# Two transformer blocks on one core: gates and branch projections computed with the weights as the moving operand

## The chip, the cores and the metric

The kernel runs on one core of a Trainium2 chip. The metric is the device time of one execution in microseconds (us); the median of three runs is compared. Engines are called TensorE (PE, with its weight loads PEld), VectorE (DVE), ScalarE (ACT), GpSimd (POOL) and SyncE (SP).

## What the kernel must compute

The input is x of 256 rows (tokens) by 2048 columns. It passes two blocks. In each, x is normed and projected by one wide matrix into queries, keys, values and gate logits; several attentions each give a branch output o, which is projected back to 2048 columns; the branches are gated and summed, projected once more, normed and added to x. Then a feed-forward part follows. All data are float32. Cut to what matters here:

```python
# block 1: two branches, each of width 1024
gates = sigmoid(gate_logits + b_gate)                     # 256 x 4096
mixed = (g_sb * (o_sb @ w_o_sb) + g_mla * (o_mla @ w_o_mla)) @ w_out
h = h + rms_norm(mixed, norm_post_mix)
# block 2: three branches, each of width 512; gates 256 x 6144
bias = take(rel_bias_table, rel_bucket(q_pos - k_pos))    # one row of numbers per head, by distance
logits = q @ k.T * scale + bias                           # 20 heads, masked by distance
mix = ga * (ya @ w_oa) + gb * (yb @ w_ob) + gc * (yc @ w_oc)
x = x + rmsnorm(mix @ w_out, post_mix_g)
```

## The kernel before

Every weight matrix is streamed once from DRAM in pieces of [128 x 1024] float32 (512 KB), in the order of use, seven pieces ahead, by SyncE's queue (`load_piece`). Each piece is split three pieces ahead of its use into a rounded part `hi` (ScalarE, line 335) and a rest `lo` (VectorE, line 336), because TensorE multiplies a rounded float32 format; activations are split in the same way (`split_act`). A product is then hi x hi + lo x hi + hi x lo.

The work is a list of `Group`s, each a block of output columns. `run` takes them in order, piece by piece: it loads and splits ahead, multiplies, and after each piece steps the generators that evacuate earlier groups (`tail_step`) and the side generators that compute attention heads (`step`). All engines execute their instructions in the order in which this list writes them.

`multiply` has two forms. In kind "w" the weights are the stationary operand and the activations move: a piece holds 4 k-tiles of 256 output columns and gives 16 matmuls, in pairs of 512 moving columns (`hi` against both parts) and 256 (`lo` against the rounded part). The result lies in PSUM turned, with the output columns on the partitions. In kind "a" the activations stand and the weights move: a piece holds 2 k-tiles of 512 output columns and gives 12 matmuls of 512 columns; the result has the tokens on the partitions.

Before the change the gates and the branch projections are of kind "w". A gate group is evacuated by `gather` (per 256 columns two copies on ScalarE, line 851, and two additions on VectorE, line 852), scaled by the norm on GpSimd (line 860) and later turned into a sigmoid with its bias on ScalarE (`sigmoids`, line 1022). A branch group goes through `gather` too (tile `y`), is multiplied by its gate on GpSimd (line 1035) and added to the branch before it, on GpSimd as well (line 1039); the sum (tile `tr`) is then split for the output projection (`hh`, `hl`). A group of block 1's branches has four pieces, one of block 2's a single piece. PSUM holds four such result banks, two for a group, so that a group can begin when the one before the last is evacuated.

In block 2 the attention bias is one row of 384 numbers per head. `bias_rows` (run during the last down projection group of block 1) writes each row 128 times into DRAM, and `bias_tile` reads it with a row step of 383, so that each query gets its row shifted by one more place.

`renorm` adds a norm's result to x, transposes x and starts the next projection. While TensorE waits for the norm, `warm_forms` issues twelve matmuls on zeros, at the first of three norms with 128 columns, at the other two with 512 and 256 in turn.

Of the kernel before, what the change touches and what calls it, by code (L numbers as in the profile page):

```python
# [19 lines left out]
P = 128  # L20
# [24 lines left out]
G_BUFS = 63  # L45
# [47 lines left out]
def lay_out(x):  # L93
# [6 lines left out]
        + span(2048, 2) + span(0, 4, 256) + span(1024, 4, 256) + span(4416, 16, 256),  # L100
        moving=range(5),
# [5 lines left out]
    g.add("osb", x["w_o_sb"][0], span(0, 8, 256))  # L107
    g.add("omla", x["w_o_mla"][0], span(0, 8, 256))
# [11 lines left out]
        + span(2304, 4, 256) + span(3328, 1) + span(3840, 24, 256),  # L120
        moving=(4, 12),
    )
    g.add("oa", x["w_oa_2"][0], span(0, 8, 256))
    perm = [h for i in range(4) for h in (i, 4 + i)]
    ob = x["w_ob_2"][0].reshape(8, 64, D)[perm].reshape(512, D)
    g.add("ob", ob, span(0, 8, 256))
    g.add("oc", x["w_oc_2"][0], span(0, 8, 256))
# [11 lines left out]
    for name, v in [  # L139
        ("pre1", x["norm_pre_mix"][0]), ("qn", x["q_norm"][0]), ("kvn", x["kv_norm"][0]),  # L140
        ("ffn1", x["norm_pre_ffn"][0]), ("pre2", x["pre_mix_g_2"][0]), ("ffn2", x["pre_ffn_g_2"][0]),
        ("bg1", x["b_gate"][0]), ("bg2", x["b_gate_2"][0]), ("sub", x["diff_subln_g_2"][0]),
        ("cb", x["conv_b_2"][0]), ("cw0", x["conv_w_2"][0, 0]), ("cw1", x["conv_w_2"][0, 1]),
        ("cw2", x["conv_w_2"][0, 2]),
    ]:
        c = column(v)
        where[name] = n
        n += c.shape[1]
        cols.append(c)
    a["colv"] = np.ascontiguousarray(np.concatenate(cols, axis=1))  # L150
    a["rows"] = np.ascontiguousarray(
# [68 lines left out]
class Net:  # L220
    def __init__(self, ctx, tc, dram, sizes, colpos, out):
# [15 lines left out]
        self.norms = 0  # L237
# [186 lines left out]
class Blocks(Net):  # L424

    def setup(self):
# [26 lines left out]
        self.idle_r = self.const([P, 512], "idle_r", F32R)  # L453
        nc.vector.memset(self.idle_r.bitcast(F32), 0.0)
# [14 lines left out]

    def warm_forms(self, which):  # L470

        t = self.idle_r
        ps = self.aux("warm")
        two = lambda x: x.rearrange("p (r b) -> p b r", r=2)
        out = lambda x: x.rearrange("p (b r) -> p b r", r=2)
        plain = [t[:, 0:P], t[:, P : 2 * P]]
        turned = [t[:, a : a + 2 * P].rearrange("p (b r) -> p r b", r=2)[:, 0] for a in (0, P)]
        full, half, few = two(t), two(t)[:, 0:P], two(t)[:, 0:64]
        jobs = [
            [(plain[i % 2], few, P) for i in range(6)] + [(turned[i % 2], few, P) for i in range(6)],  # L480
            [(plain[i % 2], (full, half)[i % 2], (512, T)[i % 2]) for i in range(12)],
            [(turned[i % 2], (full, half)[i % 2], (512, T)[i % 2]) for i in range(12)],
        ][which]
        for i, (lhs, rhs, n) in enumerate(jobs):
            self.nc.tensor.matmul(out(ps[:, 0:n]), lhsT=lhs, rhs=rhs, start=i == 0, stop=i == 11, skip_group_check=True)
# [31 lines left out]
    def broadcast_r(self, diag, qscale):  # L517
# [59 lines left out]
    def renorm(self, first, gname, qscale, update=True, twin=None):  # L577
# [38 lines left out]
        def broadcast():  # L616
            diag = self.diagonal(self.rpre)
            yield
            self.broadcast_r(diag, qscale)
            self.r_ready = True  # L620
# [97 lines left out]
    def turn(self, e):  # L718
# [6 lines left out]
        nc.vector.tensor_copy(pt, ps[:, 0:384])  # L725
# [28 lines left out]
    def bias_tile(self, h):  # L754
        m = self.mpool.tile([P, T], F32, tag="m", name=self.name("m"))
        src = bass.AP(self.bias.tensor, self.bias.offset + h * P * 384 + 127, [[383, P], [1, T]])
        self.nc.gpsimd.dma_start(m, src)
        return m

    def diff_head(self, h):  # L760
# [20 lines left out]
        w = self.turn(es[0])  # L781
# [19 lines left out]
    def soft_pair(self, qs, ks, masks, vs, out, i, name, floors=None, sinks=None):  # L801
# [17 lines left out]
        for j in range(2):  # L819
            ws.append(self.turn(es[j]))  # L820
            yield
# [20 lines left out]
    def gather(self, ps, name, scale=None, n=2):  # L842
# [3 lines left out]
        for i in range(n):  # L846
# [15 lines left out]
    def gathered(self, ps, name, rb, n=2):  # L862

        o = self.gather(ps, name, n=n)
# [6 lines left out]
    def evac_cols(self, store, i, mult):  # L871

        def f(ps):
            if mult is None or isinstance(mult, float):
                o = self.gather(ps, "tr", mult)
            else:
                o = yield from self.gathered(ps, "tr", mult)
# [138 lines left out]
    def sigmoids(self, gates, bname, n):  # L1016

        for p in range(n):
            while ("pair", p) not in gates:
# [3 lines left out]
            if p % 2:  # L1023
                yield

    def branch_evac(self, b, j, nb, gates):
# [3 lines left out]
        def evac(ps):  # L1030
            p = 8 * b + j
            g = gates["pair", p]
            y = self.gather(ps, "y")
            yield
            nc.gpsimd.tensor_tensor(g, g, y, op=OP.mult)  # L1035
# [6 lines left out]
            yield  # L1042
            self.split_pair(g, self.mix, j)
# [53 lines left out]
    def mix_out(self, branches, gates, key_out, row):  # L1097
# [3 lines left out]
        for j in range(8):  # L1101
            for b, (key, o) in enumerate(branches):
                gs.append(Group(key, j, lambda k, o=o: o[k], self.branch_evac(b, j, len(branches), gates)))
# [4 lines left out]
    def block1(self):  # L1108
# [28 lines left out]
        gs[-1].after = lambda: self.add_side(heads + [self.sigmoids(gates, "bg1", 16)])  # L1137
        gs += [Group("in1", 13 + i, u, self.evac_cols(gates, i, self.rbc)) for i in range(16)]
# [7 lines left out]
    def bias_rows(self):  # L1146
# [13 lines left out]
        self.bias = self.tc.dram_tile([20, P, 384], F32, name="bias")  # L1160
        nc.gpsimd.dma_start(self.bias, mask[0:20, None, 0:384].to_broadcast([20, P, 384]))
# [33 lines left out]
    def block2(self):  # L1195
# [24 lines left out]
        def mobas():  # L1220
# [5 lines left out]
            self.add_side(gens + [self.sigmoids(gates, "bg2", 24)])  # L1226

        gs = [
            Group("in2", 0, u, self.evac_cols(dq, 0, self.rbq)),
            Group("in2", 1, u, self.evac_cols(dq, 1, self.rbq)),  # L1230
# [3 lines left out]
            Group("in2", 5, u, self.evac_cols(sq, 0, self.rbq)),  # L1234
            Group("in2", 6, u, self.evac_cols(sq, 1, self.rbq)),
            Group("in2", 7, u, self.evac_sw, after=windows),
            Group("in2", 8, u, self.evac_cols(bq, 0, self.rbq)),
            Group("in2", 9, u, self.evac_cols(bq, 1, self.rbq)),
# [4 lines left out]
        self.renorm(gs[0], "pre2", -0.125, twin=gs[1])  # L1243
        gs += [Group("in2", 13 + i, u, self.evac_cols(gates, i, self.rbc)) for i in range(24)]
# [34 lines left out]
```

## Time and profile before

| | before |
|---|---|
| median of three runs | 2639.85 us (2639.09 to 2640.11) |
| the profiled execution | 2639.83 us, its span 2638.1 us |
| TensorE busy | 2599.4 us, 99% of the span |
| VectorE busy | 1719.2 us, 65% |
| ScalarE busy | 1410.7 us, 53% |
| GpSimd busy | 499.0 us, 19% |
| DRAM read | 510.35 MB, 196 GB/s over the span |

The span is the time from the first to the last instruction; the rest of the execution's time lies around it. Records of matmuls overlap, since they are pipelined, so a busy TensorE is not one at its peak: the distance from one start to the next tells more than the length of a record.

### The profile page before, as it was taken

How to read it: one execution, taken by the hardware profiler on the slowest of the kernel's cores; microseconds unless marked ns; L12 is line 12 of the kernel's file. 1: busy time of each engine (PE TensorE's matmuls, PEld its weight loads, DVE VectorE, ACT ScalarE, POOL GpSimd, SP SyncE). 2: the span in 40 equal slices, each digit the busy share in tenths (PEclk: the TensorE clock that was granted, in tenths of full speed). 3: DMA queues.
4: the chain of work that ended last, by engine and by line, in shares of the span. 5: the costliest groups of instructions: out<-in, count | busy, mean ns of one | idle time of the engine just before them, and what ended most of it. 6: DMA issues, size and time to landing. Idle time of an engine off the chain costs nothing.

```text
span 2638.1 us, 38603 instructions
## 1 busy us (share of the span) xinstructions
PE 2599.4 (99%) x14802; PEld 2337.2 (89%) x14802; DVE 1719.2 (65%) x2187; ACT 1410.7 (53%) x2189; POOL 499.0 (19%) x371
## 2 busy tenths in 40 slices
PE   9999999999999999999999999998999999999997
PEld 7898899988999999888889889997889999998886
DVE  6656666856666666544467676568578788786454
ACT  5547465546555555444355456555466666665443
POOL 0010011401222222200021111129123222221000
PEclk9999999999999999999999999999999999999999
DMA  7665556675666666766755665665756666666664
GB/s 242 195 191 161 163 176 199 201 222 169 200 202 202 198 204 201 223 208 202 246 178 173 190 197 183 202 195 171 223 155 215 204 202 201 201 202 220 202 200 150
DMA packets 144777, 518.91 MB, mean 197 GB/s; under 512 B 16980, under 2 KB 17390, under 8 KB 144592
## 3 DMA queue, kind: packets, MB, share of 16 engines
q1 hardware_dynamic: 140544, 505.07, 61.8%
q0 software_dynamic: 3904, 11.37, 1.6%
q8 instruction: 115, 1.88, 0.3%
q14 instruction: 70, 0.57, 0.1%
q10 hardware_dynamic: 144, 0.01, 0.0%
HBM read 510.35 MB, written 6.03 MB: 196 GB/s over the span
## 4 chain that ended last, share of the span: by engine, by line
PE 89%; issue 4%; POOL 3%; DVE 2%; DMA 1%; ACT 1%; SPq 0%; DVEq 0%; ACTq 0%; POOLq 0%
PE mm L421 86%; POOL tr L1035 1%; POOL tr L1039 1%; DMA raw<-w_dn 1%; PE s L689 1%; DVE lo L336 1%; PE o L675 0%; PE tr L543 0%; PE pt L723 0%; DVE res L572 0%; ACT hi L335 0%; POOL res L575 0%; DMA raw<-w_in 0%; PE o L676 0%; ACT u L536 0%
## 5 line engine op out<-in xcount | busy, mean ns | idle before, releaser
L336 DVE TENSOR_TENSOR lo<-raw,hi 128x1024 fp32r<-128x1024 f32 (+1 forms) x957 | 1293.0, 1353 | 738.0 <-ACT hi L335 735.3
L421 PE MATMUL mm<-u,hi 128*128 128x512 f32 x4704 | 1554.6, 384 | 0.2
L335 ACT CAST hi<-raw 128x1024 fp32r<-128x1024 f32 (+1 forms) x957 | 998.6, 1047 | 763.8 <-PE mm L421 634.7
L421 PE MATMUL mm<-u,lo 128*128 128x256 f32 x4704 | 1283.0, 273 | 0.7 <-DVE lo L336 0.7
L421 PEld LDWEIGHTS mm<-u,hi 128*128 128x128 f32 x4704 | 889.8, 189 | 125.7 <-issue 1.0
L421 PEld LDWEIGHTS mm<-u,lo 128*128 128x128 f32 x4704 | 903.7, 192 | 1.4 <-DVE lo L336 1.3
L421 PE MATMUL mm<-hi,h 128*128 128x512 f32 x1408 | 419.8, 379 | 0.6 <-ACT hi L335 0.6
L421 PEld LDWEIGHTS mm<-hi,h 128*128 128x128 f32 x1408 | 266.1, 189 | 38.7 <-ACT hi L335 1.0
L421 PE MATMUL mm<-lo,h 128*128 128x512 f32 x704 | 267.3, 380 | 2.7 <-DVE lo L336 2.7
L851 ACT COPY low<-mm 128x256 f32<-128x256 f32 x382 | 132.2, 374 | 170.8 <-PE mm L421 169.6
L860 POOL TENSOR_TENSOR tr<-tr,rbc 128x512 f32<-128x512 f32 x48 | 63.4, 1320 | 541.8 <-DVE tr L852 541.8
L421 PEld LDWEIGHTS mm<-lo,h 128*128 128x128 f32 x704 | 133.0, 189 | 23.4 <-DVE lo L336 4.5
L421 PE MATMUL mm<-hi,u 128*128 128x512 f32 (+1 forms) x448 | 133.2, 374 | 1.4 <-ACT hi L335 1.4
L1082 POOL TENSOR_TENSOR cc<-cc 128x256 f32<-128x256 f32 x44 | 68.2, 1550 | 292.9 <-DVE cc L1075 262.6
L492 POOL TENSOR_TENSOR r<-st,mhalf 128x2 f32<-128x2 f32 x14 | 11.8, 849 | 576.5 <-DVE st L491 576.5
L860 POOL TENSOR_TENSOR gu<-gu,rbc 128x512 f32<-128x512 f32 x44 | 57.4, 1306 | 244.1 <-DVE gu L852 241.2
L421 PE MATMUL mm<-lo,hh 128*128 128x512 f32 x256 | 97.1, 379 | 0.0
L421 PE MATMUL mm<-hi,hh 128*128 128x512 f32 x256 | 97.0, 379 | 0.0
L421 PE MATMUL mm<-hi,hl 128*128 128x512 f32 x256 | 97.0, 379 | 0.0
L421 PEld LDWEIGHTS mm<-hi,u 128*128 128x128 f32 x448 | 83.8, 191 | 12.4 <-ACT hi L335 2.1
L421 PE MATMUL mm<-lo,u 128*128 128x512 f32 (+1 forms) x224 | 83.2, 371 | 1.1 <-DVE lo L336 1.1
L1075 DVE SCALAR_TENSOR_TENSOR cc<-cu,colv,cc 128x255 f32<-128x255 f32 (+1 forms) x176 | 81.2, 483 | 3.1
(224 smaller groups left out, 2010.4 us busy)
## 6 DMA issues: line engine op xcount, KB each, us to landing
raw<-w_in SPq DMA_DIRECT2D x284, 512.0 KB, 4.2
raw<-w_gu SPq DMA_DIRECT2D x176, 512.0 KB, 4.3
raw<-w_dn SPq DMA_DIRECT2D x176, 512.0 KB, 4.3
raw<-w_up SPq DMA_DIRECT2D x176, 512.0 KB, 4.2
raw<-w_out SPq DMA_DIRECT2D x64, 512.0 KB, 4.3
raw<-w_osb SPq DMA_DIRECT2D x16, 512.0 KB, 4.2
raw<-w_omla SPq DMA_DIRECT2D x16, 512.0 KB, 4.1
raw<-w_ukv SPq DMA_DIRECT2D x8, 512.0 KB, 4.3
```

The costliest lines, as they stand in the source:

```text
L335: self.nc.scalar.copy(hi[:, :n], raw[:, :n])
L336: self.nc.vector.tensor_tensor(lo[:, :n], raw[:, :n], hi[:, :n].bitcast(F32), op=OP.subtract)
L421: self.nc.tensor.matmul(out, lhsT=lhs, rhs=rhs, start=start, stop=stop, skip_group_check=True)
L492: self.nc.gpsimd.tensor_tensor(r, y, self.mhalf[:, 0:w], op=OP.pow)
L689: nc.tensor.matmul(s[:, c : c + w], lhsT=q[:, qs], rhs=k[:, 0:w], start=start and i == 0, stop=i == n - 1, skip_group_check=True,)
L851: nc.scalar.copy(lc, b)
L860: self.nc.gpsimd.tensor_tensor(o3, o3, rb[:, None, :].to_broadcast([P, n, T]), op=OP.mult)
L1035: nc.gpsimd.tensor_tensor(g, g, y, op=OP.mult)
L1039: nc.gpsimd.tensor_tensor(g, g, gates["pair", p - 8], op=OP.add)
L1075: nc.vector.scalar_tensor_tensor(cn[:, s:T], un[:, 0 : T - s], self.col(w, k), cn[:, s:T], op0=OP.mult, op1=OP.add)
L1082: nc.gpsimd.tensor_tensor(g, g, v, op=OP.mult)
```

## The change

Gates and branch projections become kind "a", with 512 columns to a group; their weights are laid out for that on the host. A gate group is evacuated by VectorE alone, which scales by the norm and adds the gate bias; the bias is loaded as a row broadcast to all partitions when the group starts, on GpSimd's queue. A branch group is evacuated by VectorE alone, which multiplies PSUM by the gate. The sum over branches stays on GpSimd. Since the sum now has tokens on the partitions, TensorE turns it by transposes for the output projection. The bias rows of block 2 are written once, and `bias_tile` reads them with a row step of 1; for that the queries of these heads are stored in reverse order, and the attention weights are put back in order when they are turned. `warm_forms` gives way to `warm(12)`, which has twelve bf16 matmuls of 512 columns. The pool of general tiles grows from 63 to 64.

```diff
-        + span(2048, 2) + span(0, 4, 256) + span(1024, 4, 256) + span(4416, 16, 256),
-        moving=range(5),
+        + span(2048, 2) + span(0, 4, 256) + span(1024, 4, 256) + span(4416, 8),
+        moving=(*range(5), *range(13, 21)),
...
-    g.add("osb", x["w_o_sb"][0], span(0, 8, 256))
+    g.add("osb", x["w_o_sb"][0], span(0, 4), moving=range(4))
...
-                self.warm_forms(self.norms)
-                self.norms += 1
+                self.warm(12)
...
-            nc.vector.tensor_scalar(self.rbq, ps[:, 0:T], qscale, None, op0=OP.mult)
+            form = lambda x: x.rearrange("p (t b) -> p t b", t=NT)
+            nc.vector.tensor_scalar(form(self.rbq)[:, :, ::step], form(ps[:, 0:T]), qscale, None, op0=OP.mult)
...
-        nc.vector.tensor_copy(pt, ps[:, 0:384])
+        form = lambda x: x.rearrange("p (a b) -> p a b", a=3)
+        nc.vector.tensor_copy(form(pt), form(ps[:, 0:384])[:, :, ::step])
...
-        src = bass.AP(self.bias.tensor, self.bias.offset + h * P * 384 + 127, [[383, P], [1, T]])
+        src = bass.AP(self.bias.tensor, self.bias.offset + h * 384, [[1, P], [1, T]])
...
-                nc.vector.tensor_tensor(oc, a, lc, op=OP.add)
+                nc.vector.tensor_tensor(oc[:, :, ::step], a, lc, op=OP.add)
...
+    def gate_groups(self, key, gates, first, row, n):
...
+            def pre():
+                bias.append(self.g("bg"))
+                src = self.dram["bgates"][0:1, row + i * 512 : row + (i + 1) * 512].partition_broadcast(P)
+                nc.gpsimd.dma_start(bias[0], src)
+
+            def evac(ps):
+                tiles = []
+                for t in range(NT):
+                    o = self.g("gt")
+                    nc.vector.scalar_tensor_tensor(o, ps[t], self.rpre[:, t : t + 1], bias[0], op0=OP.mult, op1=OP.add)
+                    tiles.append(o)
+                gates[i] = tiles
...
-            for i in (2 * p, 2 * p + 1):
-                self.nc.scalar.activation(gates[i], gates[i], AF.Sigmoid, bias=self.col(bname, i))
...
+            for o in gates[i]:
+                self.nc.scalar.activation(o, o, AF.Sigmoid)
...
-            p = 8 * b + j
-            g = gates["pair", p]
-            y = self.gather(ps, "y")
-            yield
-            nc.gpsimd.tensor_tensor(g, g, y, op=OP.mult)
+            m = gates[4 * b + j]
+            for t in range(NT):
+                nc.vector.tensor_tensor(m[t], ps[t], m[t], op=OP.mult)
             if not b:
                 return
             yield
-            nc.gpsimd.tensor_tensor(g, g, gates["pair", p - 8], op=OP.add)
+            for t in range(NT):
+                nc.gpsimd.tensor_tensor(m[t], m[t], gates[4 * b - 4 + j][t], op=OP.add)
             if b < nb - 1:
                 return
-            yield
-            self.split_pair(g, self.mix, j)
+            for _ in range(3):
+                yield
+            for q in range(2):
+                tr = self.aux("mt")
+                for n in range(2):
+                    c = slice((2 * q + n) * P, (2 * q + n + 1) * P)
+                    for t in range(NT):
+                        o = n * T + t * P
+                        nc.tensor.transpose(tr[:, o : o + P], m[t][:, c], self.ident)
+                self.split_pair(tr, self.mix, 2 * j + q)
+                yield
...
-        self.bias = self.tc.dram_tile([20, P, 384], F32, name="bias")
-        nc.gpsimd.dma_start(self.bias, mask[0:20, None, 0:384].to_broadcast([20, P, 384]))
+        self.bias = self.tc.dram_tile([20, 384], F32, name="bias")
+        nc.gpsimd.dma_start(self.bias, mask[0:20, 0:384])
```

## Rows read from the trace of the kernel before

**Rows 1.** The page: busy time of each engine, its share, instructions.
```profile
PE 2599.4 (99%) x14802; PEld 2337.2 (89%) x14802; DVE 1719.2 (65%) x2187; ACT 1410.7 (53%) x2189; POOL 499.0 (19%) x371
```
**Rows 2.** The page: the chain that ended last, by line.
```profile
PE mm L421 86%; POOL tr L1035 1%; POOL tr L1039 1%; DMA raw<-w_dn 1%; PE s L689 1%; DVE lo L336 1%; PE o L675 0%; PE tr L543 0%; PE pt L723 0%; DVE res L572 0%; ACT hi L335 0%; POOL res L575 0%; DMA raw<-w_in 0%; PE o L676 0%; ACT u L536 0%
```
**Rows 3.** Busy time by stretch: branches of block 1; block 2: heads, gates, branches.
```profile
447.00:531.00 84.00, 84.00 (x515) 77.22 (x514) 69.42 (x71) 47.92 (x74) 38.46 (x27) 1.00 0.65 199
1500.00:1610.00 110.00, 109.82 (x703) 96.81 (x702) 77.31 (x162) 55.93 (x112) 14.45 (x16) 1.00 0.58 182
1620.00:1768.00 148.00, 148.00 (x906) 136.13 (x905) 90.81 (x86) 82.45 (x121) 17.92 (x14) 1.00 0.67 204
1768.00:1842.00 74.00, 65.82 (x392) 58.72 (x391) 60.13 (x79) 42.26 (x80) 67.27 (x36) 1.00 0.55 169
```
**Rows 4.** Timeline of TensorE, gates of block 2: first and last of 17 starts.
```profile
1650.02 0.38 PE L421 MATMUL mm<-u,hi 128*128 128x512 f32 x1
...
1652.64 0.38 PE L421 MATMUL mm<-u,hi 128*128 128x512 f32 x1
```
**Rows 5.** Timeline of TensorE, output projection of block 1: first and last of 13.
```profile
580.04 0.38 PE L421 MATMUL mm<-hi,hh 128*128 128x512 f32 x1
...
582.63 0.38 PE L421 MATMUL mm<-hi,hh 128*128 128x512 f32 x1
```
**Rows 6.** Timeline of TensorE around four transposes between two pieces, block 1.
```profile
87.85 0.60 PE L967 MATMUL lt<-cmat,nat 128*128 128x128 f32 x4
88.20 0.46 PE L421 MATMUL mm<-hi,u 128*128 128x512 f32 x1
88.50 0.38 PE L421 MATMUL mm<-lo,u 128*128 128x512 f32 x1
```
**Rows 7.** By tile: first and last start in block 2's branch projections.
```profile
L421 PE MATMUL mm<-oa,hi x64: 382/382/382, 1768.6 to 1834.2; 128*128 128x512 f32 x64
L421 PE MATMUL mm<-oc,lo x64: 272/273/273, 1774.8 to 1841.4; 128*128 128x256 f32 x64
```
**Rows 8.** Timeline of one wait in block 2's branch projections.
```profile
1795.72 0.62 ACT L533 CAST hh<-tr 128x512 fp32r<-128x512 f32 x1 [3.20 <-POOL tr L1039]
...
1797.39 0.74 DVE L852 TENSOR_TENSOR y<-mm,low 128x256 f32<-128x256 f32 x2
...
1797.85 0.48 PE L421 MATMUL mm<-ob,hi 128*128 128x512 f32 x1 [1.45 <-DVE y L852]
```
**Rows 9.** Groups by line from 1768 to 1838 us: busy, mean ns.
```profile
L336 DVE TENSOR_TENSOR lo<-raw,hi 128x1024 fp32r<-128x1024 f32 x23 | 36.4, 1582 | 5.6 <-ACT hi L335 5.6
L1039 POOL TENSOR_TENSOR tr<-tr,tr 128x512 f32<-128x512 f32 x13 | 27.0, 2074 | 1.0
```
**Rows 10.** Groups by line, whole span: the nearest evacuation by VectorE.
```profile
L561 DVE TENSOR_TENSOR mg<-mm,gain 128x512 f32<-128x512 f32 x32 | 20.6, 686 | 12.0 <-PE mm L421 12.0
```
**Rows 11.** DMA issues from 1262 to 1304 us: KB each, median us to landing.
```profile
raw<-w_dn SPq DMA_DIRECT2D x12, 512.0 KB, 11.9
bias<-bm POOLq DMA_DIRECT2D x1, 3840.0 KB, 38.3
```
**Rows 12.** TensorE's waits from 1262 to 1304 us: total, times, longest.
```profile
PE mm L421 <- DVE lo L336: 2.7, 4, 0.8
PE mm L421 <- ACT hi L335: 0.6, 1, 0.6
```
**Rows 13.** Busy time by stretch: 18 us after the first and the second norm.
```profile
617.00:635.00 18.00, 17.11 (x100) 15.03 (x101) 15.50 (x25) 11.60 (x22) 5.09 (x3) 0.91 0.25 75
1322.17:1340.17 18.00, 16.97 (x107) 14.83 (x108) 16.57 (x27) 12.65 (x24) 5.20 (x3) 1.00 0.29 93
```
**Rows 14.** Timeline: a split while GpSimd is idle; an add and the split behind it.
```profile
609.81 1.23 DVE L336 TENSOR_TENSOR lo<-raw,hi 128x1024 fp32r<-128x1024 f32 x1 [1.36 <-ACT hi L335]
...
1783.84 1.28 POOL L1039 TENSOR_TENSOR tr<-tr,tr 128x512 f32<-128x512 f32 x1
1784.02 2.18 DVE L336 TENSOR_TENSOR lo<-raw,hi 128x1024 fp32r<-128x1024 f32 x1 [0.53 <-ACT hi L335]
```

More of the change, by code (lines that the diff above doesn't have):

```diff
@@ L44 @@
 TWO_PI = _two_pi()
-G_BUFS = 63
+G_BUFS = 64
 PIECE = 1024
@@ L106, in lay_out @@
     g.add("ukv", x["w_ukv"][0], ukv, moving=(4, 5))
-    g.add("osb", x["w_o_sb"][0], span(0, 8, 256))
-    g.add("omla", x["w_o_mla"][0], span(0, 8, 256))
+    g.add("osb", x["w_o_sb"][0], span(0, 4), moving=range(4))
+    g.add("omla", x["w_o_mla"][0], span(0, 4), moving=range(4))
     g.add("out1", x["w_out"][0], span(0, 4), moving=range(4))
@@ L468, in warm @@
             self.nc.tensor.matmul(ps.rearrange("p (a b) -> p a b", a=4), lhsT=self.idle, rhs=rhs, start=True, stop=True)
[L470 to L485, printed above, removed]
     def rstd(self, ss, n, w=NT):
@@ L575, in residual, with renorm @@
             self.nc.gpsimd.tensor_tensor(h, h, m, op=OP.add)
-    def renorm(self, first, gname, qscale, update=True, twin=None):
+    def renorm(self, first, gname, qscale, update=True, twin=None, step=1):
         self.u = [None] * KD
@@ L716, in divide, with turn @@
             self.nc.vector.tensor_scalar(e[:, a : a + w], e[:, a : a + w], c[:, i : i + 1], None, op0=OP.mult)
-    def turn(self, e):
+    def turn(self, e, step=1):
         nc = self.nc
@@ L780, in diff_head @@
             yield
-        w = self.turn(es[0])
+        w = self.turn(es[0], -1)
         yield
@@ L819, in soft_pair @@
         for j in range(2):
-            ws.append(self.turn(es[j]))
+            ws.append(self.turn(es[j], -1))
             yield
@@ L876, in f @@
             else:
-                o = yield from self.gathered(ps, "tr", mult)
+                o = yield from self.gathered(ps, "tr", mult, step=step)
             for n in range(2):
@@ L1014, in split_pair, with group, sigmoids @@
             store[2 * i + n] = (hi[:, c], lo[:, c], None)
-    def sigmoids(self, gates, bname, n):
-        for p in range(n):
-            while ("pair", p) not in gates:
+    def gate_groups(self, key, gates, first, row, n):
+        nc = self.nc
+        def group(i):
+            bias = []
+            def pre():
[9 more added lines that the diff above has]
+                gates[i] = tiles
+            return Group(key, first + i, lambda k: self.u[k], evac, "a", pre)
+        return [group(i) for i in range(n)]
+    def sigmoids(self, gates, n):
+        for i in range(n):
+            while i not in gates:
                 yield
-            for i in (2 * p, 2 * p + 1):
-                self.nc.scalar.activation(gates[i], gates[i], AF.Sigmoid, bias=self.col(bname, i))
-            if p % 2:
-                yield
+            for o in gates[i]:
+                self.nc.scalar.activation(o, o, AF.Sigmoid)
+            yield
     def branch_evac(self, b, j, nb, gates):
@@ L1100, in mix_out @@
         gs = []
-        for j in range(8):
+        for j in range(4):
             for b, (key, o) in enumerate(branches):
-                gs.append(Group(key, j, lambda k, o=o: o[k], self.branch_evac(b, j, len(branches), gates)))
+                gs.append(Group(key, j, lambda k, o=o: o[k], self.branch_evac(b, j, len(branches), gates), "a"))
         outs = [Group(key_out, j, lambda k: self.mix[k], self.post_evac(j), "a") for j in range(4)]
@@ L1136, in block1 @@
         heads = [self.mla_pair(i) for i in range(4)]
-        gs[-1].after = lambda: self.add_side(heads + [self.sigmoids(gates, "bg1", 16)])
-        gs += [Group("in1", 13 + i, u, self.evac_cols(gates, i, self.rbc)) for i in range(16)]
+        gs[-1].after = lambda: self.add_side(heads + [self.sigmoids(gates, 8)])
+        gs += self.gate_groups("in1", gates, 13, 0, 8)
         mixes, outs = self.mix_out([("osb", self.o_sb), ("omla", self.o_mla)], gates, "out1", 0)
@@ L1242, in block2 @@
         ]
-        self.renorm(gs[0], "pre2", -0.125, twin=gs[1])
-        gs += [Group("in2", 13 + i, u, self.evac_cols(gates, i, self.rbc)) for i in range(24)]
+        self.renorm(gs[0], "pre2", -0.125, twin=gs[1], step=-1)
+        gs += self.gate_groups("in2", gates, 13, 4096, 12)
         mixes, outs = self.mix_out([("oa", self.o_a), ("ob", self.o_b), ("oc", self.o_c)], gates, "out2", 2)
```

44 lines of the change are left out of this document (21 added, 23 removed).

## The prediction

> **What bounds the kernel now.** I read the totals first: TensorE is busy 2599.4 of 2638.1 us, VectorE 65%, ScalarE 53%, GpSimd 19% [rows 1]. The chain of work that ended last agrees: 86% of it is the matmul of line 421 [rows 2]. A gain must therefore take TensorE time away or close a hole in it. So I next cut the span into stages. In the gate stage of block 2 TensorE is busy 148.00 of 148 us; in the branch projections of block 1, 84.00 of 84 us. In those of block 2 it is busy 65.82 of 74 us, with GpSimd at 67.27 us [rows 3]. That one stage has a hole, and in it another engine is the fullest. "Busy" can't rank two matmul forms, because records overlap (0.38 us each, started 0.22 us apart), so I take start-to-start times from the timeline.
>
> **The change part by part.**
>
> *Weights moving instead of standing, 216 pieces.* A piece of 512 KB is 16 matmuls in the old form: from 1650.02 to 1652.64 us, 8 pairs, 2.62 us [rows 4]. In the form that the change uses, which the output projections already have, it is 12 matmuls of 512 columns: 580.04 to 582.63 us, 2.59 us [rows 5]. The changed pieces are 64 gate pieces in block 1, 96 in block 2, 32 branch pieces in block 1 and 24 in block 2, together 216, the same number before and after. 216 x 0.03 = **-6.5 us**. The starts are printed to 0.01 us, so the term lies between -4 and -9.
>
> *Turning the gated sum, 64 transposes.* Before, the sum came out turned; now each block turns 16 x 2 tiles on TensorE, in 16 bursts of four, each between two pieces. Such a burst stands in the trace: four transposes start at 87.85, the next matmul at 88.20, and the one after it only at 88.50, 0.30 instead of 0.216 us later [rows 6]. A burst thus costs 0.35 + 0.09 = 0.44 us, and 16 x 0.44 = **+7.0 us**. Without the slow restart it would be 5.6, the lower end. The two parts so far cancel.
>
> The Trainium skill ("TensorE: Matmul & The Clock Gate", Part 4) puts a 128x128 transpose at about 275 ns in a kernel's context. This trace shows four within 0.35 us, so by spacing the page's figure does not hold here; by that page 64 of them would cost 17.6 us.
>
> *The hole in block 2's branch projections.* The 24 pieces run from 1768.6 to 1841.5 us (last start 1841.4 plus the start spacing), 72.9 us [rows 7], where 24 x 2.62 = 62.9 is the matmul work: 10.0 us of hole. Its cause is in one column block: ScalarE's cast of the sum waits 3.20 us for GpSimd's add and starts at 1795.72; behind it on ScalarE stand the copies out of PSUM, behind those VectorE's add at 1797.39, and TensorE gets its bank at 1797.85 after 1.45 us idle [rows 8]. The change takes the 24 multiplications off GpSimd here (to VectorE, straight from PSUM) and the PSUM copies off ScalarE. GpSimd keeps 16 adds of [128x512] at 2.07 us [rows 9], 33 us in place of 67. A PSUM bank is then freed by VectorE alone, 0.69 us per tile by the nearest row, also [128x512] from PSUM with a second operand [rows 10]. The turn is held back four pieces after the group's end, 10.4 us, while the multiply and the two adds it waits for take 1.4 + 4.1 us; what is queued behind it on TensorE is the out projection or the next branch, and neither waits. So **-10.0 us**; the other end is in the first rival.
>
> *VectorE there.* Per column block (6 pieces, 6 x 2.59 + 0.88 = 16.4 us of TensorE) it has 6 splits at 1.58 us [rows 9] = 9.5, 6 multiplications = 4.1, and 2 splits of the turned sum, which have half the columns of a weight split and are estimated at half its time, = 1.6: 15.2 us. That is 93% full, but under the bound.
>
> *Bias rows stored once.* The 3840 KB write takes 38.3 us to land, and beside it the median weight piece, an eighth of its size, takes 11.9 us [rows 11], where TensorE uses one up in 2.6. TensorE then waits five times, 3.3 us [rows 12]. Each wait also hides 0.38 - 0.22 us of the previous record and brings a slow restart (0.48 for 0.38 us, as in [rows 8]): 3.3 + 5 x 0.26 = 4.6. The write shrinks to 30 KB: **-4.6 us**; at least 3.3. The reads stay 20 of 128 KB.
>
> *Warming.* Twelve bf16 matmuls of 512 columns replace twelve others. They run while TensorE waits for the norm, so they cost nothing if they fit that wait, as the old ones do; spaced like the 512-column matmuls they take 12 x 0.216 = 2.6 us. At half the clock they would take 5.2, and with all of the 2.6 more on the path it would be +7.8 at three norms; I take nothing. What the first norm may gain is the clock: over the 18 us from its first transposes the granted clock averages 0.91 of 2.4 GHz (a stretch of it at the lower level, 1.2), against 1.00 at the second norm, and TensorE starts 100 matmuls against 107 [rows 13]. The first warms with 128-column matmuls, the second with 512 and 256, the new ones have 512. Seven matmuls at 2.62 / 16 us are **-1.1 us**; 0 is the other end, and 0.09 x 18 = 1.6 the most.
>
> *At nothing.* The gates' copies, adds, scaling and sigmoids shrink on ScalarE, VectorE and GpSimd, but no TensorE time hangs on them: 148.00 of 148 us [rows 3]. The 20 gate bias loads of 256 KB are issued on GpSimd's queue one group (8 pieces, 20.7 us) ahead; even the 512 KB pieces beside the bias write landed in 11.9. Reversed queries put a step of -1 on 12 additions and 20 copies of VectorE; no row has such a step. In the heads' stage VectorE is busy 77.3 of 110 us [rows 3] and splits weights three pieces ahead, so even at twice their length (some 0.5 us more each, 16 us over about 220) they stay covered; without that cover it would be +16.
>
> **Sum.** -6.5 + 7.0 - 10.0 - 4.6 - 1.1 = -15.2 us. The profiled execution took 2639.83 us (span 2638.1 and 1.7 around it), which is the median of the three runs, 2639.85, within 0.02. Forecast: 2639.8 - 15.2 = **2624.6 us**.
>
> **The rivals.**
>
> *Two engines at one port.* VectorE becomes the bound of block 2's branch stage. For it: a split takes 1.23 us while GpSimd is idle, but one that starts 0.18 us after an add takes 2.18, as if it had waited for the add's end [rows 14]. If each of the four adds of a column block held up a split for its whole 1.28 us, VectorE would need 6 x 1.23 + 4.1 + 1.6 + 4 x 1.28 = 18.2 us against 16.4, a hole of 7.2 us over four: 2631.8 us. Against it: that takes four adds which each start just before a split; the average split of this stage is 1.58 us with GpSimd busy nine tenths of the time, and GpSimd will be busy half of it. It decides where VectorE passes 16.4 us, at an average split of 1.78. The Trainium skill ("SBUF — State Buffer", SBUF: two separate sides) has the rule: the port pair that VectorE and GpSimd share is an exclusive lock for operations with two SBUF inputs; whoever starts first holds it and the other waits. The split of 2.18 us agrees.
>
> *No gain in the matmul form.* If the gates' 12 matmuls run no faster than the old 16, and the clock falls as before, it is 2624.6 + 6.5 + 1.1 = 2632.2 us. Against it: 2.59 is steady over the output projections.
>
> *Transposes that don't overlap.* If each burst waited for the matmul before it to drain (0.38 - 0.22 us) and held TensorE for its whole record of 0.60 us, with the slow restart, it would cost 0.85 us: 13.6 instead of 7.0, 2631.2 us. Against it: the next matmul starts 0.35 us after the burst does [rows 6]. This is the page's rule on transposes above, as far as rows carry it.
>
> *Gate biases late, slower than before.* VectorE's evacuation of a gate group waits for its bias row; behind it stand the weight splits, and for them TensorE. It decides once a load lands later than 20.7 us plus the three split pieces, 7.8 us, after its issue: 28.5 us. To turn the sum to +0.2% it must cost 15.2 + 5.3 = 20.5 us, about 1.0 us in each of 20 groups, so 2645 us at landings of 29.5 us. Against it: 11.9 us for twice the size in the most crowded window of this trace.
>
> **How the numbers follow.** 0.2%, 5.3 us, is about what a measurement here can tell from no change, so faster means under 2634.5. The forecast with its bounds (the matmul form -4 to -9, the burst without restart -1.4, bias 3.3, clock 0, a VectorE remainder up to 2) runs from 2620 to 2629 and gets 0.60. The port gets 0.17, no gain in the form 0.08, both faster. Transposes that don't overlap get 0.03, also faster; two of these together, which end within 0.2%, get 0.06. Late biases, or a warming that overruns on top of another, get 0.06. Faster is thus 0.88. The range 2620 to 2633 holds the first three but for their edges.
>
> **What would show it.** The branch stage of block 2 with TensorE idle under 2 us and GpSimd near 33 us; pieces 2.59 us apart in the gate stages; bursts of four "mt" transposes at 0.44 us; no wait for splits near the end of the first down projection; a granted clock of 1.00 after the first norm. It is wrong if VectorE's splits hold TensorE in the branch stage, or if waits on the gate bias or on the reversed copies stand in the heads' stage.

## The result and the profile after

The changed kernel takes 2622.57 us (median of four runs, 2622.42 to 2623.61) against 2639.98 us for the kernel before (four runs): a ratio of 0.9935, with a 95% interval of 0.9921 to 0.9948. The forecast was 2624.6 us, range 2620 to 2633. The profiled execution took 2623.61 us, its span is 2621.6.

The page of the changed kernel, the counterpart of [rows 1] and [rows 2]: busy time by engine, and the chain by engine.

```profile
PE 2599.2 (99%) x14002; PEld 2309.1 (88%) x14002; DVE 1674.4 (64%) x2106; ACT 1354.8 (52%) x1989; POOL 382.8 (15%) x311
...
PE 96%; DVE 1%; ACT 1%; issue 1%; POOL 1%; DMA 0%; SPq 0%; DVEq 0%; ACTq 0%; POOLq 0%
```

TensorE's busy time is the same, 2599 us, in a span 16.5 us shorter. That says little by itself, since records overlap. So compare where each stage begins. The next table is read from the starts of TensorE's instructions in both traces: each stage runs from the first start of its own work to that of the next. The stages that it leaves out differ by no more than 0.12 us each; together they give back 0.2 us.

| stage | before | after | difference |
|---|---|---|---|
| start to first matmul on the latents | 197.41 | 196.87 | -0.54 |
| block 1: after the last latent matmul, heads and gates | 191.53 | 189.64 | -1.89 |
| block 1: branch projections | 83.84 | 85.51 | +1.67 |
| block 1: output projection | 82.88 | 83.76 | +0.88 |
| first norm, transposes to broadcast | 35.66 | 34.55 | -1.11 |
| first feed-forward part, up | 432.73 | 432.73 | 0.00 |
| first down projection, to the warming | 233.40 | 228.57 | -4.83 |
| block 2: first scores to last head | 212.09 | 210.65 | -1.44 |
| block 2: gates after the last head | 160.12 | 158.30 | -1.82 |
| block 2: branch projections | 72.94 | 64.79 | -8.15 |
| block 2: output projection | 83.15 | 83.76 | +0.61 |

What the change doesn't touch repeats to the hundredth (432.73). Three stages grew, all with transposes of the gated sum in them: block 1's branch projections and the output projections of both blocks, over whose first pieces the last of these transposes fall. Block 2's branch projections have them too, but lost more by the hole that closed.

Busy time by stretch in the changed kernel, the counterpart of [rows 3] (columns: stretch, its length, then PE, PEld, DVE, ACT, POOL, clock, DMA share, GB/s): block 1's branches, block 2's heads, gates, branches.

```profile
444.50:530.00 85.50, 85.50 (x409) 74.92 (x408) 54.32 (x55) 37.66 (x40) 12.62 (x10) 1.00 0.63 208
1500.00:1610.00 110.00, 110.00 (x568) 91.90 (x569) 73.98 (x154) 54.78 (x102) 9.64 (x18) 1.00 0.63 206
1605.00:1755.00 150.00, 150.00 (x696) 131.35 (x695) 79.70 (x72) 72.67 (x80) 0.00 (x0) 1.00 0.65 203
1759.54:1824.34 64.80, 64.80 (x314) 56.79 (x312) 54.22 (x54) 29.30 (x32) 24.42 (x14) 1.00 0.59 189
```

In the last row TensorE has no hole any more, and GpSimd fell from 67.27 of 74 us [rows 3] to 24.42 of 64.80. The groups by line of that stage (columns: busy, mean ns, idle before):

```profile
L336 DVE TENSOR_TENSOR lo<-raw,hi 128x1024 fp32r<-128x1024 f32 x24 | 38.0, 1591 | 6.6 <-ACT hi L335 6.3
L1045 POOL TENSOR_TENSOR gt<-gt,gt 128x512 f32<-128x512 f32 x14 | 24.5, 1770 | 204.6 <-DVE gt L1040 204.6
L1040 DVE TENSOR_TENSOR gt<-mm,gt 128x512 f32<-128x512 f32 x22 | 14.1, 679 | 0.0
L516 DVE TENSOR_TENSOR hl<-mt,hh 128x512 fp32r<-128x512 f32 x6 | 4.1, 685 | 4.0 <-ACT hh L515 4.0
```

The adds (line 1045) take 1.77 us rather than 2.07, the splits stay at 1.59, and the multiplications out of PSUM take 0.68, as their nearest row had it [rows 10].

TensorE's timeline, gates of block 2: the first and the thirteenth of the starts, 12 matmuls or 2.60 us apart (2.62 for 16 in [rows 4]).

```profile
1649.68 0.38 PE L421 MATMUL mm<-lo,u 128*128 128x512 f32 x1
...
1652.28 0.38 PE L421 MATMUL mm<-lo,u 128*128 128x512 f32 x1
```

TensorE's timeline at one of the 16 bursts of transposes: as in [rows 6], 0.35 us to the next matmul and 0.30 from that to the one after it.

```profile
475.58 0.60 PE L1056 MATMUL mt<-cmat,gt 128*128 128x128 f32 x4
475.93 0.46 PE L421 MATMUL mm<-hi,omla 128*128 128x512 f32 x1
476.23 0.38 PE L421 MATMUL mm<-lo,omla 128*128 128x512 f32 x1
```

DMA issues of the changed kernel from 1262 to 1304 us, the counterpart of [rows 11] (KB each, median us to landing). TensorE waits for nothing in this stretch.

```profile
raw<-w_dn SPq DMA_DIRECT2D x13, 512.0 KB, 3.5
...
bias<-bm POOLq DMA_DIRECT2D x1, 30.0 KB, 3.4
```

### The profile page after: what moved, and what is told of

Same layout as the page of the kernel before. It is cut to its first block, busy times and chain, and to the rows that moved or that the text cites. A ratio compares the mean times of both kernels' runs of the same rounds, so it can differ in the third digit from the quotient of the medians.

```text
span 2621.6 us, 36702 instructions
## 1 busy us (share of the span) xinstructions
PE 2599.2 (99%) x14002; PEld 2309.1 (88%) x14002; DVE 1674.4 (64%) x2106; ACT 1354.8 (52%) x1989; POOL 382.8 (15%) x311
## 4 chain that ended last, share of the span: by engine, by line
PE 96%; DVE 1%; ACT 1%; issue 1%; POOL 1%; DMA 0%; SPq 0%; DVEq 0%; ACTq 0%; POOLq 0%
PE mm L421 93%; PE s L670 1%; PE o L656 0%; PE tr L525 0%; PE pt L704 0%; DVE lo L336 0%; DVE res L554 0%; POOL res L557 0%; PE mt L1056 0%; ACT u L518 0%; PE o L657 0%; DMA res<-x_nat 0%; POOL cu L844 0%; DVE cc L1090 0%; PE z L630 0%
## 5 line engine op out<-in xcount | busy, mean ns | idle before, releaser
L421 PE MATMUL mm<-u,hi 128*128 128x512 f32 x3424 | 1126.5, 383 | 0.3
L421 PE MATMUL mm<-u,lo 128*128 128x256 f32 x3424 | 933.4, 273 | 0.5 <-DVE lo L336 0.5
L421 PEld LDWEIGHTS mm<-u,hi 128*128 128x128 f32 x3424 | 647.1, 189 | 91.3 <-DVE u L519 1.1
L421 PEld LDWEIGHTS mm<-u,lo 128*128 128x128 f32 x3424 | 657.4, 192 | 0.9 <-DVE lo L336 0.8
L421 PE MATMUL mm<-hi,u 128*128 128x512 f32 (+1 forms) x1728 | 527.3, 381 | 0.0
L421 PEld LDWEIGHTS mm<-hi,u 128*128 128x128 f32 x1728 | 325.9, 190 | 46.3 <-issue 1.4
L421 PE MATMUL mm<-lo,u 128*128 128x512 f32 (+1 forms) x864 | 325.9, 377 | 0.8 <-DVE lo L336 0.8
L421 PEld LDWEIGHTS mm<-lo,u 128*128 128x128 f32 x864 | 163.9, 190 | 22.3 <-DVE lo L336 1.6
L835 ACT COPY low<-mm 128x256 f32<-128x256 f32 x222 | 77.2, 374 | 97.5 <-PE mm L421 96.6
L1045 POOL TENSOR_TENSOR gt<-gt,gt 128x512 f32<-128x512 f32 x24 | 41.0, 1733 | 385.0 <-DVE gt L1040 385.0
```

The source lines that it names most:

```text
L421: self.nc.tensor.matmul(out, lhsT=lhs, rhs=rhs, start=start, stop=stop, skip_group_check=True)
L1045: nc.gpsimd.tensor_tensor(m[t], m[t], gates[4 * b - 4 + j][t], op=OP.add)
```

## The experiments

Profiled runs are compared stage by stage, since an untouched stage repeats to 0.1 us; ratios are to the kernel before.

### The hole in block 2's branch stage: throughput of GpSimd, or order on ScalarE

The prediction showed the hole at ScalarE, where a cast that waits for GpSimd stands in front of the PSUM copies [rows 8]. The change removed both the load on GpSimd and that order, so two edits separate them. First the load alone, put back into the changed kernel:

```diff
             for t in range(NT):
-                nc.vector.tensor_tensor(m[t], ps[t], m[t], op=OP.mult)
+                y = self.g("y")
+                nc.vector.tensor_copy(y, ps[t])
+                nc.gpsimd.tensor_tensor(m[t], m[t], y, op=OP.mult)
```

> The changed kernel with the multiplication by the gate put back on GpSimd: VectorE copies PSUM to SBUF, GpSimd multiplies and adds. ScalarE still has no copy out of PSUM there. Theory A, GpSimd's throughput made the hole in block 2's branch stage (24 multiplications and 16 adds at 1.9 to 2.1 us are 77 us against 65 us of TensorE): the stage and the first pieces after it lose 8 to 12 us again, now at the transposes, 2631 to 2635 us. Theory B, the hole came from the order on ScalarE (a cast waiting for GpSimd in front of the PSUM copies): PSUM is freed by VectorE alone, so the stage stays near 64.8 us and the kernel at 2623 to 2625 us.

Measured: 2632.21 us (0.9973, interval 0.9963 to 0.9983). All stages before are unchanged; the branch stage grows by 4.76 us and the output projection by 5.22. TensorE's waits from 1759 to 1920 us:

```profile
PE mt L1058 <- POOL gt L1047: 5.5, 4, 2.2
```

and the groups by line in the branch stage:

```profile
L336 DVE TENSOR_TENSOR lo<-raw,hi 128x1024 fp32r<-128x1024 f32 x24 | 46.6, 1960 | 3.5 <-ACT hi L335 3.2
L1042 POOL TENSOR_TENSOR gt<-gt,y 128x512 f32<-128x512 f32 x22 | 40.4, 1857 | 172.3 <-DVE y L1041 172.2
...
L1047 POOL TENSOR_TENSOR gt<-gt,gt 128x512 f32<-128x512 f32 x12 | 21.9, 1849 | 0.0
```

The transposes wait for GpSimd's adds. The load alone makes TensorE wait, without any copy on ScalarE. VectorE is not what changed: its copy takes 0.68 us, as its multiplication did. The loss, 10.0 us, is as large as the hole before, but only 5.5 us of it are waits. Behind the longest two of them the granted clock fell to its lower level; the first is in this stretch (columns as above, the clock third from the end):

```profile
1800.00:1810.00 10.00, 7.63 (x31) 5.95 (x30) 7.54 (x6) 2.33 (x3) 9.84 (x7) 0.83 0.41 143
```

There matmuls start 0.43 instead of 0.22 us apart, and the two places cost some 3.3 us (an estimate from the starts). The rest was not taken apart, so that the sum is again 10 us is in part chance. The splits rise to 1.96 us while GpSimd is fuller. That fits the first rival's two engines at one port, but TensorE has no wait for a split here.

Then the order alone, in the kernel before:

```diff
-            yield
+            for _ in range(4):
+                yield
             self.split_pair(g, self.mix, j)
```

> The kernel before with one edit: the split of the gated sum is held back three more pieces, so that ScalarE's cast no longer stands in front of the PSUM copies while GpSimd still adds. Theory A (GpSimd's throughput, 20 multiplications at 1.85 and 13 adds at 2.07 us in 70 us): the hole of 10.0 us stays within 2 us, in place or moved a few pieces later, 2638 to 2640 us. Theory B (order on ScalarE): the hole goes, 2630 us. In between, the two share it.

Measured: 2641.05 us (1.0004, interval 0.9994 to 1.0013), 1 us above theory A's range. The branch stage shrinks from 72.94 to 66.43 us, and the output projection grows from 83.15 to 91.11. Waits of TensorE from 1766 to 1926 us, first in the kernel before, then in this one:

```profile
PE mm L421 <- DVE y L852: 8.2, 7, 1.5
```
```profile
PE mm L421 <- ACT hh L533: 4.9, 1, 4.9
PE mm L421 <- DVE y L852: 1.9, 6, 0.5
```

Most of the hole moved behind the stage, into one wait of 4.9 us, because the last sum comes late from GpSimd. The cast that TensorE waits for, and the clock of the stretch behind it:

```profile
1855.90 0.62 ACT L533 CAST hh<-tr 128x512 fp32r<-128x512 f32 x1 [7.43 <-POOL tr L1039]
```
```profile
1855.00:1860.00 5.00, 3.43 (x8) 2.75 (x9) 3.05 (x3) 2.51 (x3) 0.87 (x1) 0.59 0.50 179
```

The order on ScalarE accounts for 8.2 - 6.8 = 1.4 us of the waits and decided where they lay; GpSimd's load makes the rest. The two stages together even take 1.45 us more than before (157.54 against 156.09), since behind the long wait 14 matmuls start 0.43 instead of 0.22 us apart, some 3 us (an estimate from the starts). Several short waits, as before, had left the clock at 1.00 [rows 3].

### The bias rows

```diff
-        self.bias = self.tc.dram_tile([20, 384], F32, name="bias")
-        nc.gpsimd.dma_start(self.bias, mask[0:20, 0:384])
+        self.bias = self.tc.dram_tile([20, P, 384], F32, name="bias")
+        nc.gpsimd.dma_start(self.bias, mask[0:20, None, 0:384].to_broadcast([20, P, 384]))
...
-        src = bass.AP(self.bias.tensor, self.bias.offset + h * 384, [[1, P], [1, T]])
+        src = bass.AP(self.bias.tensor, self.bias.offset + h * P * 384, [[1, P], [1, T]])
```

> The changed kernel with one edit: each bias row is again written 128 times (3840 KB), and the reads take the first copy. Theory: the write alone crowds out the weight loads at the end of block 1, so the stretch from the first matmul of the first down projection to the warming before block 2's norm grows from 228.6 to 233.4 us (+4.8), and nothing else moves: 2627.4 us. Rival: the gain came from the shorter reads or the reversed order, and the 128-fold write costs nothing by itself: 2622.6 us. A third reading, that the write matters only together with the other traffic of the old kernel, would give something between.

Measured: 2628.11 us (0.9956, interval 0.9941 to 0.9971). The stretch to the warming is 233.31 us, +4.74; every later stage is as in the changed kernel. (The median rose by 5.5 us; in the profiles the other 0.8 lies in the start, of which more below.) DMA issues from 1261 to 1304 us, and TensorE's waits from 1255 to 1310:

```profile
raw<-w_dn SPq DMA_DIRECT2D x13, 512.0 KB, 11.7
bias<-bm POOLq DMA_DIRECT2D x1, 3840.0 KB, 37.8
```
```profile
PE mm L421 <- DVE lo L336: 3.4, 5, 0.8
```

The write alone does it; the forecast's way from 3.3 us of waits to 4.6 us of time holds (3.4 to 4.74).

### The form of the gate matmuls

The edit puts the gates' weight layout, groups, scaling and sigmoids back as they were, under the new branch products:

```diff
-        gs += self.gate_groups("in2", gates, 13, 4096, 12)
+        gs += self.gate_groups_w("in2", gates, 13, 24)
...
+            def evac(ps):
+                o = yield from self.gathered(ps, "tr", self.rbc)
+                gates["pair", p] = o
+                if p % 2:
+                    gates[p // 2] = [gates["pair", p - 1], o]
```

> The changed kernel with the gates (not the branches) back in the old form: weights standing, 256 columns to a group, gathered, scaled on GpSimd, sigmoid with the bias as a column. The gates then lie turned against the branch products, so this kernel leaves out that match and its time alone is read. Theory: 160 pieces go from 2.59 to 2.62 us, +4.8 to +5.5 us over the gate stages (block 1 from 189.6 to 191.5 us between the last matmul on the latents and the first branch piece, block 2 from 158.3 to 160.1 us after the last head), 2627.5 us. Rival 1: the forms are equal and the gain of the gate stages came from less work on ScalarE, VectorE and GpSimd in the heads' stages: the pure gate stretch after the last head stays at 158.3 and only the stretch with heads grows. Rival 2: no change, 2622.6 us.

Measured: 2629.29 us (0.9960, interval 0.9945 to 0.9974). The stages return to the values of before: block 1's heads and gates to 191.53 us, block 2's heads to 212.09, its gates after the last head to 160.12: +1.89, +1.44, +1.82, together 5.15 for 160 pieces, 0.032 each. That is 0.030 in the two stretches without block 2's heads and 0.041 for the 35 pieces among them, where TensorE waits twice for a split, 0.5 us, against once, 0.3 us: so some 0.4 us of the 5.15 seem not to be the form's. The start of this profile is another 1.0 us longer (below). The second interval decides against rival 1: after the last head the stretch is 158.30 us with the new form and 160.12 with the old, and TensorE is fully busy in both. Busy time in that stretch, changed kernel and this one:

```profile
1601.60:1759.40 157.80, 157.80 (x732) 138.19 (x733) 83.74 (x77) 77.71 (x85) 0.00 (x0) 1.00 0.64 203
```
```profile
1606.00:1765.00 159.00, 159.00 (x973) 146.26 (x973) 94.93 (x92) 91.51 (x137) 20.13 (x15) 1.00 0.64 200
```

VectorE, ScalarE and GpSimd do 11, 14 and 20 us more here, but TensorE waits for none of them; the difference goes with the form of its matmuls, 973 against 732 records.

To see what the 0.03 us hang on, the old form was reordered where the changed kernel still has it:

```diff
-                    jobs.append((n * 512, 2 * T, hi[:, kk, cs], two(both), False))
-                    jobs.append((n * 512 + T, T, lo[:, kk, cs], mh, end))
+                for n in range(width // P):
+                    jobs.append((n * 512, 2 * T, hi[:, kk, cs(n)], two(both), False))
+                for n in range(width // P):
+                    jobs.append((n * 512 + T, T, lo[:, kk, cs(n)], mh, end))
```

> The changed kernel with the matmuls of the old form reordered: both 512-column matmuls of a k-tile first, then both 256-column ones, in place of 512, 256, 512, 256. It asks where the 0.03 us per piece of the old form come from, and whether the 876 half-pieces or so that still have this form can get some of it back (3504 pairs at 2.5 ns are 8.8 us). Theory: the 2.5 ns hang on each change from a 512-column matmul to a 256-column one, so half of them go, 3504 x 1.2 ns = -4.4 us, with 2.61 us to a piece of the feed-forward part: 2618 us. Rival: the weight load (0.19 us long) needs a long matmul in front of it; two matmuls of 0.11 us in a row then leave TensorE waiting for weights, up to 0.08 us for each second one, 1752 x 0.08 = +140 us at the most. A third reading, no change, says that the 2.5 ns belong to each pair whatever its order.

Measured: 2622.17 us (0.9939, interval 0.9922 to 0.9956), the feed-forward stretch again 432.73 us. TensorE's timeline in it: four k-tiles, 16 matmuls, from 800.21 to 802.83 us.

```profile
800.21 0.60 PE L422 MATMUL mm<-u,hi 128*128 128x512 f32 x2
800.64 0.38 PE L422 MATMUL mm<-u,lo 128*128 128x256 f32 x2
800.86 0.60 PE L422 MATMUL mm<-u,hi 128*128 128x512 f32 x2
...
802.83 0.38 PE L422 MATMUL mm<-u,hi 128*128 128x512 f32 x1
```

The third reading holds, neither theory nor rival: 2.62 us to a piece in either order, so nothing is to be had by this one. That the cost goes with the number of matmuls, 16 against 12 for the same columns, fits; it was not told apart from the 256-column matmuls, which only the old form has.

### The transposes

```diff
-                tr = self.aux("mt")
-                for n in range(2):
...
-                        nc.tensor.transpose(tr[:, o : o + P], m[t][:, c], self.ident)
-                self.split_pair(tr, self.mix, 2 * j + q)
+                self.split_pair(m[q], self.mix, 2 * j + q)
```

> The changed kernel without the 64 transposes: the gated sum is split as it lies, so the sum isn't turned. Theory: 16 bursts at 0.44 us go, -7.0 us, 3.5 us in each block's branch stage with the first pieces of its out projection: 2615.5 us. Rival 1: bursts hide behind matmuls that are still draining and cost only their 4 x 0.07 to 0.09 us without a restart, -4.5 to -5.6 us: 2617.5 us. Rival 2: a burst holds TensorE for its 0.60 us record and the drain, 0.85 us: -13.6 us, 2609 us.

Measured: 2616.75 us (0.9913, interval 0.9897 to 0.9930). The median lies between the theory and rival 1, so the stages decide: each block's branch stage loses 2.63 us and its output projection 0.88, together 7.02 us. The branch stage of block 2 without turning:

```profile
1756.33:1818.49 62.16, 62.16 (x289) 54.43 (x288) 55.70 (x54) 29.47 (x32) 24.96 (x15) 1.00 0.63 198
```

62.16 us are 24 x 2.59: with the hole gone and no transposes, nothing but the pieces is left.

Both bursts of a column block in one:

```diff
-            for q in range(2):
-                tr = self.aux("mt")
+            trs = [self.aux("mt") for _ in range(2)]
+            for q in range(2):
                 for n in range(2):
...
-                self.split_pair(tr, self.mix, 2 * j + q)
-                yield
+            for q in range(2):
+                self.split_pair(trs[q], self.mix, 2 * j + q)
```

> The changed kernel with the eight transposes of a column block in one burst instead of two bursts of four a piece apart. Theory: a burst costs 4 x 0.09 plus one slow restart of 0.08 us, so eight restarts go, -0.7 us: 2621.9 us, and each burst with its restart takes about 0.79 us beyond the matmul before it. Rival: the second half of a burst must wait for nothing but the splits of 16 columns blocks come bunched, and VectorE's splits of the weights come late: +1 us or more with waits on the weight splits in block 2's branch stage.

Measured: 2622.05 us (0.9937, interval 0.9922 to 0.9952); the stages are 85.51 and 64.79 us, as with two bursts. The theory fell. TensorE's timeline at a burst of eight:

```profile
476.12 1.04 PE L1056 MATMUL mt<-cmat,gt 128*128 128x128 f32 x8
476.91 0.46 PE L421 MATMUL mm<-hi,omla 128*128 128x512 f32 x1
```

Eight take 0.79 us to the next start, where four take 0.35. With 0.11 us to each of the others, the last one has only 0.03 in front of the next matmul, and that one is late by 0.08: the two cancel. A transpose costs 0.11 us of TensorE, in bursts of four as of eight.

### Reversed queries, and the warming

The step of -1 was undone in the two kinds of places (`evac_cols`, `turn`) and in `renorm`:

```diff
-        w = self.turn(es[0], -1)
+        w = self.turn(es[0])
...
-            Group("in2", 0, u, self.evac_cols(dq, 0, self.rbq, -1)),
+            Group("in2", 0, u, self.evac_cols(dq, 0, self.rbq)),
```

> The changed kernel with step +1 in place of -1: queries in natural order, so the bias rows don't belong to their queries, and the copies that turn the attention weights run forwards. Theory: the step costs nothing; copies of [128x384] out of PSUM take 0.55 us and additions 0.42 us either way, and the time stays at 2622.6 us within 0.5. Rival: VectorE reads or writes backwards more slowly (twice the time would be 16 us of VectorE over the heads' stages), and undoing it shortens those records and takes up to 2 us off the waits for splits in the heads' stage.

Measured: 2623.33 us (0.9940, interval 0.9926 to 0.9955). The heads' stage is 210.64 us against 210.65, and the copies that turn the weights take 552 ns in both (20 of these 28 run backwards in the changed kernel); the additions that evacuate 256 columns (12 of them backwards) take 418 ns on average in both. The copies' group by line, forwards:

```profile
L707 DVE COPY pt<-pt 128x384 f32<-128x384 f32 x28 | 15.4, 552 | 1.6 <-PE pt L704 1.6
```

The step costs nothing.

The warming at the first norm, with 128 columns:

```diff
-                self.warm(12)
+                (self.warm if self.norms else self.warm_narrow)(12)
+                self.norms += 1
```

> The changed kernel with one edit: at the first of the three norms the twelve warming matmuls have 128 columns (bf16), as the old ones there had (rounded float32), instead of 512. Theory: the granted clock falls for a stretch after the first norm as before the change, and the stretch from its first transposes to the norm's broadcast grows from 34.55 to 35.66 us (+1.1): 2623.7 us. Rival: the lower clock came from the old data type or form, and narrow bf16 warming keeps the clock at 1.00 and the stretch at 34.55 us.

Measured in a single run: 2624.58 us; the stretch after the first norm is 35.38 us, +0.83. TensorE's timeline after the norm, first of the changed kernel, then of this one:

```profile
613.77 2.76 PE L466 MATMUL warm<-idle 128*128 128x512 bf16 x12
617.27 1.73 PE L525 MATMUL tr<-cmat,res 128*128 128x128 f32 x8 [0.73 <-DVE res L554]
```
```profile
613.95 0.84 PE L474 MATMUL warm<-idle 128*128 128x128 bf16 x12
617.44 2.09 PE L532 MATMUL tr<-cmat,res 128*128 128x128 f32 x8 [2.65 <-DVE res L561]
```

Busy time of the stretch behind it, in the same order:

```profile
617.20:635.20 18.00, 16.93 (x107) 14.81 (x108) 16.59 (x27) 12.56 (x24) 5.25 (x3) 1.00 0.27 94
```
```profile
617.20:635.20 18.00, 17.03 (x101) 15.03 (x102) 15.84 (x25) 11.73 (x23) 5.10 (x3) 0.91 0.25 75
```

With the narrow ones TensorE then stands idle for 2.65 us instead of 0.73, and the granted clock of the stretch is 0.91 again, part of it at 1.2 instead of 2.4 GHz. It is not the data type. Narrowness and the longer idle time came together in this run and were not told apart. But a wait alone can do it: in the two runs on the hole the clock fell behind waits in a stream of 512-column matmuls, the longest of them 1.87, 2.21 and 4.88 us.

## Why the prediction was right

| step | forecast | measured | from |
|---|---|---|---|
| weights moving, 216 pieces | -6.5 | -6.8 | gates 5.15 (put back: 5.15); branches of block 1 83.84 to 82.88 without turning; block 2's 24 x 0.03 |
| 64 transposes | +7.0 | +7.0 | left out: 2.63 + 0.88 in each block |
| hole in block 2's branch stage | -10.0 | -10.1 | 72.94 to 62.16 without turning, less 0.72 for the form |
| bias rows once | -4.6 | -4.8 | stage table; put back: 4.74 |
| clock after the first norm | -1.1 | -1.1 | stage table; narrow warming: 0.83 |

The measured terms sum to -15.8 us; -0.3 more lies in block 2's output projection (82.88 us without turning against 83.15 before) and -0.5 in the start, and the stages left out of the table give back 0.2: the profiled span fell by 16.5.

Every step held in its place and its sign. Of the 6.8 us of the first term some 0.4 are not the matmul form but, it seems, a wait less for splits beside block 2's heads. The prediction read the hole's cause off one wait, at ScalarE's cast, and took GpSimd's load and ScalarE's copies away together without telling them apart; the experiments give most of it to the load. What was mis-sized is small. GpSimd's 16 adds were put at 33 us; in the stage it is busy 24.4, because two of the 16 fall behind it and an add takes 1.77 us on average instead of 2.07. VectorE was put at 93% of the stage and is at 84% (54.22 of 64.80 us); two multiplications and two splits of the turned sum fall behind the stage, and such a split takes 0.69 us, not 0.79. The burst's 0.44 us was right, but its division into 0.35 and a slow restart of 0.09 was not: bunching saves nothing.

The rivals. *Two engines at one port* did not come true at this load: the splits average 1.59 us, under the 1.78 at which it was to decide. With 24 more multiplications on GpSimd they went to 1.96, but even there TensorE waited for GpSimd's adds and for no split, so what this rival would cost no run shows. *No gain in the matmul form* is refuted by putting the gates back. *Transposes that don't overlap* is refuted by leaving them out: 7.0, not 13.6 us. *Gate biases late*: TensorE has no wait for them, and the page gives a median of 4.6 us from issue to landing where 28.5 would have mattered (the longest is 6.3):

```profile
bg<-bgates POOLq DMA_DIRECT2D x20, 256.0 KB, 4.6
```

The median came out 2.0 us under the forecast. The profiled execution, 2623.61 us, accounts for 1.0 of it, nearly as the terms above have it. The other 1.0 us is that the three other runs of the changed kernel have spans 1.0 to 1.2 us shorter than the profiled one; where, no trace shows. The start can do as much: the time from the first instruction to the first matmul on the latents is 196.87 us in this profile and lay between 195.3 and 197.9 in those of the experiments, of which only the reordered matmuls touch that stretch. Part of this is the clock. The first 15 us, first of the run with forward queries (195.32 us), then of that with bursts of eight (197.41):

```profile
0.00:15.00 15.00, 11.19 (x47) 6.77 (x48) 6.31 (x11) 7.84 (x12) 1.49 (x6) 1.00 0.87 303
```
```profile
0.00:15.00 15.00, 10.56 (x35) 5.97 (x36) 6.09 (x11) 7.03 (x9) 1.49 (x6) 0.89 0.86 301
```

In the three profiles with about 195.3 us matmuls start 0.22 us apart from 10.5 us on, in all others 0.43 apart until about 14 us. What decides between the two was not tried. So the 0.5 us that the start gave here is luck, not the change.

Of the variants that do the same work none is faster beyond this: bunched transposes and the other order of matmuls are the same, stage by stage.

## What to carry to other kernels

Where one engine is 99% busy, look for the stage in which another engine is the fullest and read the hole there; then test throughput against order, because moving the wait can move the hole without closing it, and one long wait can cost more than several short ones when the clock falls behind it. Price two forms of the same matmul work by the distance from start to start over a whole piece: here the columns were equal, and 16 matmuls against 12 made 1%. Take a forecast's small terms one by one even when they cancel: -6.5 and +7.0 were both real, and the hole, the write and the clock remained.

## What the runs showed of the hardware

- In the old form, 16 matmuls with 6144 columns take 2.62 us, in the new one 12 with as many columns 2.59, and a second order of the 512- and 256-column matmuls made no difference.
- A float32 transpose of 128x128 costs TensorE 0.11 us in a burst of four as in one of eight, although its record is 0.27 us long and the matmul after the burst starts late.
- A step of -1 on VectorE's reads of PSUM or writes to SBUF costs nothing: 552 ns for copies of [128x384] and 418 for additions of [128x256] either way.
- A 3840 KB write beside a stream of 512 KB loads took these from 3.5 to 11.7 us to landing, and although seven are on the way ahead, TensorE waited five times.
- Behind waits of TensorE in mid-stream, the longest 1.87, 2.21 and 4.88 us, the granted clock fell to its lower level and 512-column matmuls started 0.43 instead of 0.22 us apart for some microseconds; seven waits of at most 1.5 us each, 8.2 us in all, left it at 1.00.
- From one profile to another an untouched stage of 60 to 430 us repeats to 0.1 us, but the first 200 us, with the initial loads, vary by 2.6; in the profiles with the shortest start the first matmuls ran at the higher clock.
